# Expert stage: one buffer of transposed rows, three row and four result buffers, and the last scatters and late loads placed ahead of the branch of the full experts

## The chip, the cores and the metric

One core of one Trainium2 chip runs one program. The metric is the device time of one execution in microseconds (us); the time before is the median of 3 runs. PE is TensorE (PEld its weight loads), DVE VectorE, ACT ScalarE, POOL GpSimd, SP the engine that issues most DMAs; PEq, SPq and so on are the engines' sequencers, which run branches, semaphore instructions and DMA issues. L1322 is line 1322 of the kernel before.

## The reference

The reference is one inference step of a decoder with two layers on 576 tokens (512 of a prompt, 8 sequences of 8 samples), 1024 wide. Each layer normalizes and projects its input, runs three groups of recurrent heads (GLA, retention, Mamba-2), projects back with a residual and a norm, and then runs a mixture of experts: a token takes the best of 4 groups and the top 2 of the 4 experts in it. What the change touches is this last part, cut to its core:

```python
def hier_moe(h, l, p):
    ...
    top_v, top_i = lax.top_k(e_in, MOE_TOPK)
    ...
    hid = silu(einsum('nd,edf->nef', t, moe_w1[l])) * einsum('nd,edf->nef', t, moe_w3[l])
    y = einsum('nef,efd->nd', hid * combine[..., None], moe_w2[l])
...
x = layer_norm(ALPHA * x + g2 * hier_moe(h, l, p), ln2_g[l], ln2_b[l])
```

The kernel computes only the chosen experts of each token: 1152 rows (576 tokens times 2 choices) over 16 experts.

## The kernel before, in words

For each layer the kernel ranks the experts by how many rows they have and works through 16 **blocks**, one for each expert, from `experts` (L1819 on). A block b does, in this order: `gather` (L1322, POOL, an indirect DMA that brings its rows from hbuf to a row buffer X); `turn` (L1334 or, for the blocks in LIGHT, L1417: PE transposes the rows, and ACT and DVE copy them from PSUM into the transposed rows, as a high part xh, L1340, and a low part xl, L1341; light blocks have one plain copy xf, L1418); `up` twice (L1353, L1425); `hid` (L1363, L1434, a transpose of the hidden values); `down` (L1373, L1442), whose results ACT (L1375, L1443) and DVE (L1377) scale into a result buffer ys; and `scatter` (L1384, POOL, an indirect DMA from ys to the rows of ybuf in HBM). The weights of an expert are three pieces of 1 MB that SP loads (L1286) into slots that go round by threes; for the blocks that aren't light ACT and DVE split the pieces of `up` into high and low parts (whi, L328; wlo, L329).

An expert with more rows than the block takes needs more work: a second part (`b2`, or `bx` for a light block) and a third (`b3`). They stand in branches on values that the ranking left in registers (L1985, L1996, L2006, L2010 and, for the third, L1907) and run or not by the data. In the loop over b (L1964 on) the step of block b holds `up` of block b, the branch with the parts of blocks b-1, b and b+1, `turn` of block b+1, the gather of block b+2, `down` and `scatter` of block b-1, and `hid` of block b. The framework derives the waits from what each instruction reads and writes and orders the instructions of each engine itself, near this order; `issue_after` holds an instruction behind another, `declare_no_dep` takes a wait away.

The buffers of the kernel before: the row buffers of the main blocks are two, X0 and X1, by b % 2, and those of the extra parts two more; the transposed rows xs and xf are two each, by b % 2; the result buffers yss are two, main blocks by b % 2, a second part the other one. The last two blocks, 14 and 15, write their results over X0 and X1 instead and keep them: `kept`.

The scatter of a block that isn't light is made by one of two POOL instructions behind a branch on POOL (L1935): all rows, or only 64 where that will do (SSPLIT, HALF). For blocks 14 and 15 those are 88 and 82 rows, as ROWS says.

After the loop there is one more branch, L2061, for experts with still more rows (`nx > 0`, up to 4 full blocks). In this profile it isn't taken in either layer. Then comes `combine`: for each of five tiles of 128 tokens (tile 4 has 64) `pre` (L2106) adds, with PE, the two rows that the experts left for each token, read back from ybuf by `take` (L1894, two DMAs for each tile, SP); then DVE and ACT do residual and norm (L2118 to L2126). The tiles 0 and 1 are EARLY: they are read from ybuf before the last two scatters, and what blocks 14 and 15 add for them comes through PE, from `kept` and a mask `hot` (loaded from the constants at L1861, finished by DVE at L1870), in place of ybuf. For that ybuf's rows of these two tiles are zeroed at the start of each layer (L577, from bz). The other three tiles, 4, 2 and 3, are the late loads, 2.5 MB in six DMAs, behind the branch L2061; and as the body of this branch may change ybuf, it has loads of the EARLY tiles of its own. PE's first `pre` so reads a tile that is written ahead of the branch and also in its body.

The order in which the branch and the late loads stand:

```python
            with tc.If(nx > 0), ExitStack() as sI:
                ...
                for t in EARLY:
                    take(t)
            if ahead:
                ahead.split()
            for t in CORDER:
                if t not in EARLY:
                    take(t)
```

Of the kernel before, what the change touches and what calls it, by code (L numbers as in the profile page):

```python
# [9 lines left out]
F32 = mybir.dt.float32  # L10
# [10 lines left out]
D = 1024  # L21
# [20 lines left out]
GSPLIT, SSPLIT = (9,), (0, 1, 2, 3, 4, 5, 6, 7, 8, 9, 10, 11, 12, 13, 14, 15)  # L42
# [118 lines left out]
def _body(nc, tc, a, ctx, dbg):  # L161
# [404 lines left out]
    def conv(l, S, hT, sp_):  # L566
# [7 lines left out]
        for t in EARLY:  # L574
            for k in range(2):
                o = PL * k + 128 * t
                sp.dma_start(ybuf[o:o + 128], bz.rearrange("p g t -> p (g t)")[:, 0:D])  # L577
# [1241 lines left out]
    def experts(last, finish, l, x, R, tabs, slots, rqk, rv, ahead):  # L1819
# [8 lines left out]
        with ExitStack() as sE:  # L1828
            third_ = mkpool(sE, "w3rd", side="right")
            ep = mkpool(sE, "ep", side="right")  # L1830
            Xs.append(ep.tile([128, D], F32, name="X3"))
            for X in Xs[:3]:
                pool.memset(X, 0.0)
            xs = [[ep.tile([128, KD, 128], F32R, name=f"x{c}{i}") for c in "hl"] for i in range(2)]
            xf = [ep.tile([128, KD, 128], F32, name=f"xf{i}") for i in range(2)]
            hids = [ep.tile([128, 2, 128], F32, name=f"hid{i}") for i in range(4)]
            sl2 = rv.rearrange("p t d -> p (t d)")[:, D:D + 256], lp.tile([128, 2, 128], F32, name="slp2", tag="gtanh", bufs=2)
            yss = [ep.tile([128, D], F32, name=f"ys{i}") for i in range(2)]
# [6 lines left out]
            def aside(b):  # L1845
                if 2 <= b < 2 + NT:
# [3 lines left out]
                    with tc.issue_after(bl[max(k for k in range(b + 2) if k not in GSPLIT)].got.ins):  # L1850
# [28 lines left out]
            def light(b, X, pl, part, y):  # L1879
                return Light(b, tabs, scat, X, xf[b % 2], hids[b % 2 if part == 0 else 2], y, sl if part == 0 else sl2, pl, part)  # L1880
            bl = [light(b, Xs[b % 2], psp, 0, yss[b % 2]) if b in LIGHT else
                  Block(b, tabs, scat, Xs[b % 2], xs[b % 2], hids[b % 2], (yss if b < NE - 2 else Xs)[b % 2], sl, psp, ROWS[b]) for b in range(NE)]

            kept = Xs[:2]
# [4 lines left out]
            def take(t):  # L1889

                n = tp_(t)
                if t not in ys:
                    ys[t] = wraw.tile([128, 2048], F32, name="wraw", tag="raw").rearrange("p (k n) -> p k n", k=2)
                loads[t] = [sp.dma_start(ys[t][:n, k], ybuf[PL * k + 128 * t:PL * k + 128 * t + n]) for k in range(2)]  # L1894


            bx = {b: light(b, Xs[2 + b % 2], psx, 1, yss[1 - b % 2]) for b in LIGHT}
            b2 = {b: Block(NE + b, tabs, scat, Xs[2 + b % 2], (xf if b in LIGHT else xs)[b % 2], hids[2], yss[1 - b % 2], sl2, psx, plain=b in LIGHT) for b in SECOND}
            b3 = {b: Block(2 * NE + b, tabs, scat, Xs[2 + (b + (b in SOON)) % 2], (xf if b in LIGHT else xs)[b % 2], hids[3], yss[b % 2 if b not in LIGHT else 1 - b % 2],
                           sl2, psx, plain=b in LIGHT) for b in THIRD}  # L1900
# [51 lines left out]
            steps = finish(Xs[3])  # L1952
# [3 lines left out]
            pool.memset(Xs[3], 0.0)  # L1956
# [7 lines left out]
            for b in range(NE + 1):  # L1964
# [12 lines left out]
                if b + 2 in GSPLIT:  # L1977
# [383 lines left out]
```

## Time and profile before

| | |
|---|---|
| time, median of 3 runs | 1463.41 us (1459.72 to 1465.74) |
| the profiled execution's own time | 1461.71 us |
| its span, first to last instruction | 1459.9 us |
| mean granted TensorE clock | 0.919 |
| DVE busy | 831.6 us (57%) |
| ACT busy | 488.2 us (33%) |
| POOL busy | 422.8 us (29%) |
| DMA | 267.40 MB, mean 183 GB/s |

The profile is of one execution, and its times count from the start of the span. A timeline row gives the start, the duration, the engine and line, the operation with what it writes and reads, how many instructions in a row it stands for, and in brackets how long the engine had been idle before it and what ended that. The expert stage of layer 0 lies at about 480 to 685 us, that of layer 1 at about 1160 to 1405 us; behind each follows its combine, and behind the second the end.

### The profile page before, as it was taken

The page shows a single profiled execution, that of the slowest core. Times are in us where ns is not written, and L with a number is a line of the kernel's source. Part 1 is how long each engine was busy: PE and PEld are TensorE (multiplying, and loading weights), DVE is VectorE, ACT ScalarE, POOL GpSimd, SP SyncE. Part 2 cuts the span into 40 slices and gives each one's busy share as a digit, 9 for nine tenths or more (in the row PEclk, how much of TensorE's full clock was granted, in tenths as well). Part 3 has the DMA queues.
Part 4 walks back from the last instruction along what each step waited for, and adds up shares of the span by engine and source line. Part 5 has one row for each costly group of instructions (what it writes and reads, how often), then busy time and mean ns, then how long its engine had stood idle before and what let it go on. Part 6 is the DMA issues. An engine that isn't in the chain of part 4 may idle for free. (4 is left out here: it accounts for less than half of the span.)

```text
span 1459.9 us, 22701 instructions
## 1 busy us (share of the span) xinstructions
PE 1240.8 (85%) x8166; PEld 935.4 (64%) x8166; DVE 831.6 (57%) x1905; ACT 488.2 (33%) x902; POOL 422.8 (29%) x354
## 2 busy tenths in 40 slices
PE   4999999998985798898879998889997577977983
PEld 0998677775774455575579896777576353545741
DVE  0576457446989442356858546536789733123647
ACT  0552133321343233353454233323134222223512
POOL 0014112215234543211432322233314354321105
PEclk7999999999987799999989998999998599998997
DMA  9545665865262747995525310018454363674742
GB/s 312 172 145 173 215 228 202 299 207 161 68 196 87 267 178 263 376 362 173 191 68 174 90 58 34 30 45 285 157 182 144 130 254 140 243 288 195 291 160 85
DMA packets 94704, 267.40 MB, mean 183 GB/s; under 512 B 24952, under 2 KB 53530, under 8 KB 75609
## 3 DMA queue, kind: packets, MB, share of 16 engines
q1 hardware_dynamic: 84600, 246.59, 47.9%
q0 software_dynamic: 9952, 18.86, 3.7%
q8 instruction: 86, 1.41, 0.4%
q14 instruction: 66, 0.53, 0.1%
HBM read 238.42 MB, written 38.90 MB: 190 GB/s over the span
## 5 line engine op out<-in xcount | busy, mean ns | idle before, releaser
L402 PE MATMUL ps<-whi,hT 128*128 128x256 f32 (+1 forms) x640 | 188.9, 295 | 7.8 <-ACT hT L493 7.0
L403 PE MATMUL ps<-wlo,hT 128*128 128x256 f32 (+1 forms) x640 | 183.8, 287 | 1.2 <-DVE wlo L329 1.2
L404 PE MATMUL ps<-whi,hT 128*128 128x256 f32 (+1 forms) x640 | 183.5, 287 | 0.2
L402 PEld LDWEIGHTS ps<-whi,hT 128*128 128x128 f32 (+1 forms) x640 | 116.7, 182 | 21.7 <-issue 10.8
L403 PEld LDWEIGHTS ps<-wlo,hT 128*128 128x128 f32 (+1 forms) x640 | 116.8, 182 | 3.8 <-issue 2.1
L404 PEld LDWEIGHTS ps<-whi,hT 128*128 128x128 f32 (+1 forms) x640 | 116.5, 182 | 1.8 <-DVE hT L494 0.9
L392 PE MATMUL ps<-hT,whi 128*128 128x288 f32 x512 | 89.4, 297 | 0.0
L329 DVE TENSOR_TENSOR wlo<-wraw,whi 128x2048 fp32r<-128x2048 f32 x30 | 68.6, 2287 | 33.3 <-ACT whi L328 33.1
L329 DVE TENSOR_TENSOR wlo<-w3rd,whi 128x2048 fp32r<-128x2048 f32 x22 | 66.1, 3036 | 25.1 <-ACT whi L328 25.1
L1353 PE MATMUL ps<-whi,xh 128*128 128x256 f32 x384 | 60.1, 300 | 21.8 <-ACT whi L328 6.7
L392 PEld LDWEIGHTS ps<-hT,whi 128*128 128x128 f32 x512 | 75.1, 188 | 0.4 <-ACT zdt L531 0.4
L265 PE MATMUL ada<-wada,scond 128*32 128x512 f32 x384 | 56.9, 665 | 19.3 <-DMA wada<-w_ada 19.3
L1562 PE MATMUL ps<-whi,mh 128*128 128x512 f32 (+1 forms) x160 | 69.8, 436 | 3.7 <-ACT mh L1548 3.7
L1322 POOL DMA_INDIRECT qk<-hbuf,srci x32 | 33.4, 1042 | 129.1 <-PE ps L1417 47.3
L1564 PE MATMUL ps<-whi,ml 128*128 128x512 f32 (+1 forms) x160 | 67.4, 425 | 2.9 <-DVE ml L1549 2.9
L1353 PEld LDWEIGHTS ps<-whi,xh 128*128 128x128 f32 x384 | 52.1, 202 | 26.7 <-DVE xl L1341 8.4
L1563 PE MATMUL ps<-wlo,mh 128*128 128x512 f32 (+1 forms) x160 | 68.9, 431 | 0.0
L1384 POOL DMA_INDIRECT ybuf<-ys,srci x20 | 21.0, 1051 | 163.9 <-DVE ys L1377 48.1
L328 ACT ACTIVATE whi<-wraw 128x2048 fp32r<-128x2048 f32 x30 | 57.3, 1911 | 16.8 <-PE ps L392 8.3
L842 POOL TENSOR_TENSOR qh<-qx,ex 128x256 f32<-128x256 f32 x32 | 31.3, 1008 | 99.9 <-issue 82.6
L1373 PE MATMUL ps<-w3rd,hid 128*128 128x512 f32 x128 | 59.8, 610 | 0.3
L1353 PE MATMUL ps<-wlo,xh 128*128 128x256 f32 x384 | 55.5, 289 | 2.2 <-DVE wlo L329 1.9
(551 smaller groups left out, 2891.6 us busy)
## 6 DMA issues: line engine op xcount, KB each, us to landing
wada<-w_ada SPq DMA_DIRECT2D x48, 1024.0 KB
wraw<-moe_w SPq DMA_DIRECT2D x36, 1024.0 KB
slots<-moe_w SPq DMA_DIRECT2D x30, 1024.0 KB
w3rd<-moe_w SPq DMA_DIRECT2D x30, 1024.0 KB
wraw<-w_in SPq DMA_DIRECT2D x22, 1024.0 KB
wraw<-w_out SPq DMA_DIRECT2D x8, 1024.0 KB
ybuf<-bz SPq DMA_DIRECT2D x8, 512.0 KB
hbuf<-g SPq DMA_DIRECT2D x8, 512.0 KB
```

The lines of the kernel that those rows point to most:

```text
L265: pe.matmul(acc[32 * q:32 * q + 32, :], sc_[:, k, :], w[:, o:o + 512], start=(k == 0), stop=(k == KD - 1))
L328: split.hi = act.activation(hi[:, :n], raw[:, :n], AF.Copy)
L329: dve.tensor_tensor(lo[:, :n], raw[:, :n], hi[:, :n].bitcast(F32), op=ALU.subtract)
L392: pe.matmul(p[:mw, :], lhs[:, k, m0:m0 + mw], rhs[:, k, 288 * h:288 * (h + 1)], start=(k == 0 and lhs is vh and rhs is hT[0]), stop=(k == ...
L402: pe.matmul(p[:n], hT[0][:, k, xs], vh[:, k, :], start=(k == 0), stop=False)
L403: pe.matmul(p[:n], hT[0][:, k, xs], vl[:, k, :], start=False, stop=False)
L404: pe.matmul(p[:n], hT[1][:, k, xs], vh[:, k, :], start=False, stop=(k == KD - 1))
L1353: pe.matmul(p, x[:, k], v[:, k], start=(x is self.xh and v is vh and k == 0), stop=(x is self.xl and k == KD - 1))
L1373: pe.matmul(p, self.hT[:, f], v[:, f, c], start=(f == 0), stop=(f == 1))
L1562: pe.matmul(p[:n], mh[:, k, :n], vh, start=(k == 0), stop=False)
L1563: pe.matmul(p[:n], mh[:, k, :n], vl, start=False, stop=False)
L1564: o = pe.matmul(p[:n], ml[:, k, :n], vh, start=False, stop=(k == 3))
```

## The change

The change does six things. (1) The transposed rows xs and xf have one buffer each for all parts. (2) The main blocks have three row buffers by b % 3 (the third in rv, where `hot` lies too) and the gathers are issued one block earlier; the extra parts have two (Xx). (3) Four result buffers: main blocks by b % 3, second parts the fourth, third parts (b + 2) % 3. (4) The scatters of blocks 14 and 15 leave the POOL branch and always take all their rows. (5) The late loads stand ahead of the branch L2061, which is issued behind the last scatter, and its body loads all five tiles again in place of two. (6) For that, layer 0 zeroes all five tiles of ybuf; layer 1 zeroes the EARLY ones, as before.

```diff
@@ -39,7 +39,7 @@
 ROWS = [min(128, 2 * T // max(r - 1, 1)) for r in RANK]
 
 HALF = [64 if r > 80 else r for r in ROWS]
-GSPLIT, SSPLIT = (9,), (0, 1, 2, 3, 4, 5, 6, 7, 8, 9, 10, 11, 12, 13, 14, 15)
+GSPLIT, SSPLIT = (9,), tuple(range(NE - 2))
 SECOND = [b for b in range(NE) if RANK[b] < 2 + 2 * T // 129]
 SOON = (2,)
 THIRD = [b for b in range(NE) if RANK[b] < 2 + 2 * T // 257]
@@ -571,10 +571,10 @@
         bz = sp_.tile([128, 2, T], F32, name="bz")
         pool.memset(bz, 0.0)
 
-        for t in EARLY:
+        for t in (ORDER, EARLY)[l]:
             for k in range(2):
                 o = PL * k + 128 * t
-                sp.dma_start(ybuf[o:o + 128], bz.rearrange("p g t -> p (g t)")[:, 0:D])
+                sp.dma_start(ybuf[o:o + tp_(t)], bz[:tp_(t)].rearrange("p g t -> p (g t)")[:, 0:D])
         cw = cp_.tile([128, 6, 5], F32, name="cw")
         sp.dma_start(cw, a["conv_w"][l])
         dve.tensor_scalar(cw, cw, 0.5, None, op0=ALU.mult)
@@ -1828,14 +1828,16 @@
         with ExitStack() as sE:
             third_ = mkpool(sE, "w3rd", side="right")
             ep = mkpool(sE, "ep", side="right")
-            Xs.append(ep.tile([128, D], F32, name="X3"))
-            for X in Xs[:3]:
+
+            Xm, Xx = Xs, [ep.tile([128, D], F32, name=f"X{i}") for i in range(2)]
+            for X in (*Xm, Xx[1]):
                 pool.memset(X, 0.0)
-            xs = [[ep.tile([128, KD, 128], F32R, name=f"x{c}{i}") for c in "hl"] for i in range(2)]
-            xf = [ep.tile([128, KD, 128], F32, name=f"xf{i}") for i in range(2)]
+
+            xs = [ep.tile([128, KD, 128], F32R, name=f"x{c}") for c in "hl"]
+            xf = ep.tile([128, KD, 128], F32, name="xf")
             hids = [ep.tile([128, 2, 128], F32, name=f"hid{i}") for i in range(4)]
             sl2 = rv.rearrange("p t d -> p (t d)")[:, D:D + 256], lp.tile([128, 2, 128], F32, name="slp2", tag="gtanh", bufs=2)
-            yss = [ep.tile([128, D], F32, name=f"ys{i}") for i in range(2)]
+            yss = [ep.tile([128, D], F32, name=f"ys{i}") for i in range(4)]
             w3rd = third_.tile([128, 3 * 2048], F32, name="w3rd")
             w3rd = [w3rd[:, 2048 * i:2048 * (i + 1)] for i in range(3)]
 
@@ -1847,7 +1849,7 @@
                     n, xt = tp_(b - 2), x[:tp_(b - 2), b - 2]
                     st = R["stat"][:n, b - 2]
                     act.activation(xt, xt, AF.Identity, scale=st[:, 1:2], bias=st[:, 2:3])
-                    with tc.issue_after(bl[max(k for k in range(b + 2) if k not in GSPLIT)].got.ins):
+                    with tc.issue_after(bl[max(k for k in range(min(b + 3, NE)) if k not in GSPLIT)].got.ins):
                         pool.tensor_tensor(xt, xt, ln1[:n, 0], op=ALU.mult)
                         pool.tensor_tensor(xt, xt, ln1[:n, 1], op=ALU.add)
                 if b == NE - 2 and ahead:
@@ -1877,11 +1879,11 @@
                         ahead.AB = feat_ab(l + 1, lp)
 
             def light(b, X, pl, part, y):
-                return Light(b, tabs, scat, X, xf[b % 2], hids[b % 2 if part == 0 else 2], y, sl if part == 0 else sl2, pl, part)
-            bl = [light(b, Xs[b % 2], psp, 0, yss[b % 2]) if b in LIGHT else
-                  Block(b, tabs, scat, Xs[b % 2], xs[b % 2], hids[b % 2], (yss if b < NE - 2 else Xs)[b % 2], sl, psp, ROWS[b]) for b in range(NE)]
-
-            kept = Xs[:2]
+                return Light(b, tabs, scat, X, xf, hids[b % 2 if part == 0 else 2], y, sl if part == 0 else sl2, pl, part)
+
+            kept = [Xm[(NE - 1) % 3 + 1], Xm[(NE - 1) % 3]]
+            bl = [light(b, Xm[b % 3], psp, 0, yss[b % 3]) if b in LIGHT else
+                  Block(b, tabs, scat, Xm[b % 3], xs, hids[b % 2], yss[b % 3] if b < NE - 2 else kept[b - NE + 2], sl, psp, ROWS[b]) for b in range(NE)]
             hot = rv.rearrange("p t d -> p (t d)")
             loads = {}
             ys = {t: slots[i].rearrange("p (k n) -> p k n", k=2) for i, t in enumerate(CORDER[2:])}
@@ -1894,10 +1896,10 @@
                 loads[t] = [sp.dma_start(ys[t][:n, k], ybuf[PL * k + 128 * t:PL * k + 128 * t + n]) for k in range(2)]
 
 
-            bx = {b: light(b, Xs[2 + b % 2], psx, 1, yss[1 - b % 2]) for b in LIGHT}
-            b2 = {b: Block(NE + b, tabs, scat, Xs[2 + b % 2], (xf if b in LIGHT else xs)[b % 2], hids[2], yss[1 - b % 2], sl2, psx, plain=b in LIGHT) for b in SECOND}
-            b3 = {b: Block(2 * NE + b, tabs, scat, Xs[2 + (b + (b in SOON)) % 2], (xf if b in LIGHT else xs)[b % 2], hids[3], yss[b % 2 if b not in LIGHT else 1 - b % 2],
-                           sl2, psx, plain=b in LIGHT) for b in THIRD}
+            bx = {b: light(b, Xx[b % 2], psx, 1, yss[3]) for b in LIGHT}
+            b2 = {b: Block(NE + b, tabs, scat, Xx[b % 2], xf if b in LIGHT else xs, hids[2], yss[3], sl2, psx, plain=b in LIGHT) for b in SECOND}
+            b3 = {b: Block(2 * NE + b, tabs, scat, Xx[(b + (b in SOON)) % 2], xf if b in LIGHT else xs, hids[3], yss[(b + 2) % 3], sl2, psx, plain=b in LIGHT)
+                  for b in THIRD}
 
             def two(b):
                 return tc.If((beyond & (1 << b)) > 0)
@@ -1949,11 +1951,12 @@
                 q.hid()
                 q.down()
                 q.scatter()
-            steps = finish(Xs[3])
+            steps = finish(Xx[0])
             next(steps)
             bl[0].turn()
             next(steps)
-            pool.memset(Xs[3], 0.0)
+            bl[2].gather()
+            pool.memset(Xx[0], 0.0)
             with tc.issue_after(last[0].ins), tc.issue_after(last[1].ins):
                 bl[0].up()
             for i in range(2):
@@ -1974,8 +1977,8 @@
                     bl[b + 1].split(0)
                 if b < NE and b not in LIGHT:
                     bl[b].up(1)
-                if b + 2 in GSPLIT:
-                    parts(b + 2, bl[b + 2].gather, True)
+                if b + 3 in GSPLIT:
+                    parts(b + 3, bl[b + 3].gather, True)
 
                 at_hand = [e for e in (b - 1, b, b + 1) if e in SECOND and e not in LIGHT or e == b and b in LIGHT]
                 if b in SECOND and b not in LIGHT:
@@ -2031,8 +2034,8 @@
                         load(b + 3, i)
                 if b + 1 < NE:
                     bl[b + 1].turn()
-                    if b + 2 < NE and b + 2 not in GSPLIT:
-                        bl[b + 2].gather()
+                    if b + 3 < NE and b + 3 not in GSPLIT:
+                        bl[b + 3].gather()
                     if b + 1 not in LIGHT:
                         bl[b + 1].split(1)
                         if b + 4 < NE:
@@ -2044,7 +2047,7 @@
                         for t in EARLY:
                             take(t)
                     st = parts(b - 1, bl[b - 1].scatter, b - 1 in SSPLIT)[0]
-                    if b > NE - 2:
+                    if b >= NE - 1:
                         for t in EARLY:
                             for o in loads[t]:
                                 tc.declare_no_dep(st.ins, o.ins, reason="other rows")
@@ -2057,14 +2060,17 @@
                 aside(b)
 
 
+            for t in CORDER:
+                if t not in EARLY:
+                    take(t)
             wr = slots[1]
-            with tc.If(nx > 0), ExitStack() as sI:
+            with tc.issue_after(st.ins), tc.If(nx > 0), ExitStack() as sI:
                 for j in range(NX):
                     if j == 0:
                         left_over(R, wr, tabs)
                     else:
                         sI.enter_context(tc.If(nx > j))
-                    q = Block(3 * NE + j, tabs, scat, Xs[3], xf[j % 2], hids[j % 2], yss[j % 2], sl, psx, plain=True)
+                    q = Block(3 * NE + j, tabs, scat, Xx[0], xf, hids[j % 2], yss[j % 2], sl, psx, plain=True)
                     e = sp.value_load(tabs[2][0:1, j:j + 1], min_val=0, max_val=NE - 1)
                     q.w = [wr] * 3
                     q.gather()
@@ -2077,13 +2083,12 @@
                     q.down()
                     q.scatter()
                 sI.close()
-                for t in EARLY:
+                first = dict(loads)
+                for t in CORDER:
                     take(t)
+                loads.update(first)
             if ahead:
                 ahead.split()
-            for t in CORDER:
-                if t not in EARLY:
-                    take(t)
         return g2, ys, loads, kept
 
     def combine(x, tail, rv, sG, leads):
```

## Rows read from the trace of the kernel before

**Rows 1.** The page, part 1: busy time of each engine, share, instructions.
```profile
PE 1240.8 (85%) x8166; PEld 935.4 (64%) x8166; DVE 831.6 (57%) x1905; ACT 488.2 (33%) x902; POOL 422.8 (29%) x354
```

**Rows 2.** The chain that ended last: start, duration, what.
```profile
1408.87 15.43 PE ps L2106 x32
```

**Rows 3.** The list of waits, PE: us in total, times, longest.
```profile
PE ps L1353 <- ACT whi L328: 6.7, 2, 3.9
...
PE ps L1353 <- ACT xh L1340: 6.1, 2, 3.2
...
PE ps L1334 <- DMA v<-hbuf,srci: 4.0, 1, 4.0
```

**Rows 4.** Timeline of layer 1's expert loop, ACT and PE, 1241 to 1341 us.
```profile
1241.22 0.69 ACT L1375 ACTIVATE ys<-ps,wslot 128x512 f32<-128x512 f32 x1 [12.51 <-DMA ybuf<-ys,srci]
...
1241.96 3.68 PE L1442 MATMUL ps<-wraw,hid 128*64 128x512 f32 x8 [10.17 <-ACT ys L1375]
...
1245.97 2.07 PE L1353 MATMUL ps<-whi,xh 128*128 128x256 f32 x8
...
1288.74 1.19 PE L1353 MATMUL ps<-whi,xh 128*128 128x256 f32 x8
...
1340.76 1.94 PE L1442 MATMUL ps<-wraw,hid 128*64 128x512 f32 x8
```

**Rows 5.** Timeline of layer 1's hand-over: SP, DVE, POOL and PE, 1405 to 1425 us.
```profile
1405.03 4.53 SPq L318 DMA_DIRECT2D ln<-ln  x2
1415.87 3.20 SPq L1894 DMA_DIRECT2D slots<-ybuf  x6
...
1405.04 0.75 DVE L1377 TENSOR_SCALAR qk<-ps,wslot 128x512 f32<-128x512 f32 x1 [3.64 <-PE ps L1373]
...
1413.76 0.90 POOL L1384 DMA_INDIRECT ybuf<-qk,srcf  x1 [6.06 <-DMA ln<-ln]
...
1408.87 3.40 PE L2106 MATMUL ps<-wraw,cst 128*128 128x512 f32 x4 [3.87 <-SPq L2061]
...
1424.22 2.36 PE L2106 MATMUL ps<-slots,cst 64*64 64x512 f32 x5
```

**Rows 6.** Line L2061 on SP in layer 1: duration ns, first and last start.
```profile
L2061 SPq COMPARE_BRANCH  x1: 45/45/45, 1405.4 to 1405.4; - x1
...
L2061 SPq EVENT_SEMAPHORE  x6: 17/17/17, 1408.8 to 1409.1; - x6
```

**Rows 7.** Timeline of layer 0's hand-over: SP, DVE, POOL and PE, 675 to 697 us.
```profile
675.80 1.76 SPq L1894 DMA_DIRECT2D wraw<-ybuf  x4
...
693.44 3.19 SPq L1894 DMA_DIRECT2D slots<-ybuf  x6
...
683.26 0.75 DVE L1377 TENSOR_SCALAR qk<-ps,wslot 128x512 f32<-128x512 f32 x1 [2.86 <-PE ps L1373]
...
690.78 0.90 POOL L1384 DMA_INDIRECT ybuf<-qk,srcf  x1 [5.29 <-DVE x L2120]
...
685.32 1.96 PE L2106 MATMUL ps<-wraw,cst 128*128 128x512 f32 x4 [2.10 <-PEq L2061]
```

**Rows 8.** Line L2061 on SP in layer 0: all nine counters, then the first six.
```profile
L2061 SPq EVENT_SEMAPHORE  x9: 17/17/17, 680.7 to 684.7; - x9
...
L2061 SPq EVENT_SEMAPHORE  x6: 17/17/17, 680.7 to 681.1; - x6
```

**Rows 9.** Timeline of SP at layer 0's zeroing, 85 to 120 us.
```profile
88.88 3.16 SPq L577 DMA_DIRECT2D ybuf<-bz  x4
101.39 0.38 SPq L381 DMA_DIRECT2D wraw<-w_in  x1
```

**Rows 10.** Busy time by stretch: us, PE, PEld, DVE, ACT, POOL, PEclk, DMA share, GB/s.
```profile
95.00:100.00 5.00, 5.00 (x40) 5.00 (x39) 4.87 (x10) 3.31 (x7) 1.10 (x4) 1.00 0.03 10
```

**Rows 11.** Timeline of layer 0: the load of hot (SP), the transposes of block 14 (PE).
```profile
643.34 0.34 SPq L1861 DMA_DIRECT2D v<-consts  x1
...
664.66 1.03 PE L1334 MATMUL ps<-cst,qk 128*128 128x128 f32 x8
```

## The prediction, made before the changed kernel ran

> **What bounds the kernel now.** The page's engine shares come first: PE is busy for 1240.8 us, 85% of the span [rows 1], so time is won only where PE stands still, and lost where something new makes it stand. The chain of waits comes next. It ends on PE's 32 matmuls of the combine (L2106) and then on DVE [rows 2], so whatever delays the first of these matmuls delays the end one for one. The list of PE's waits [rows 3] and the timelines round them give the three places that the change touches: one stop inside the expert loop of layer 1 [rows 4], and the hand-over from the experts to the combine, in layer 1 [rows 5, 6] and in layer 0 [rows 7, 8].
>
> In rows 4 PE stands for 10.17 us ahead of block 3's down (L1442) "<-ACT ys L1375". ACT itself had sat idle for 12.51 us until a scatter of ys had landed. The reader should see that two result buffers, shared by main, second and third parts of the blocks, are what stops PE: ACT may not write block 2's result before the scatter that still reads its buffer is through.
>
> In rows 6 SP meets the branch L2061 at 1405.4. The branch isn't taken, but SP then raises the counters that the body would have raised, the last six only at 1408.8 to 1409.1: by then the ln load that SP had issued at 1405.03 [rows 5] was 3.8 us old, which I read as its landing. So at a branch not taken SP still waits for its own transfers in flight; and PE, whose first combine matmul reads a tile that the body could have written, starts at 1408.87 after 3.87 us "<-SPq L2061" [rows 5]. The late loads (slots<-ybuf, x6, from 1415.87) stand behind the branch and cost nothing: PE's matmuls on slots follow at 1424.22 with no idle time ahead of them. In layer 0 four early loads, issued from 675.80 [rows 7], hold the last of nine counters back to 684.7 [rows 8], 8.9 us after the first issue, while PE starts at 685.32, released by its own branch.
>
> The profiled execution took 1461.71 us, span 1459.9 and 1.8 round it; it lies 1.7 us below the median of 1463.41. I sum against the profiled one. A difference of 0.5%, 7.3 us, is about what a measurement of this kernel can tell from none.
>
> **The change, part by part.** *Four result buffers.* Main blocks 2 and 3 and the second and third parts of block 2 now have different buffers, so the 10.17 us go. So does the slow clock behind the stop: eight matmuls of L1442 take 3.68 us behind it and 1.94 elsewhere, the next eight of L1353 2.07 and 1.19 [rows 4]; 1.7 + 0.9 = 2.6. What is late next: block 4's down uses the third part's buffer, whose scatter has landed by 1241.22, when ACT goes on, and that is about when PE would get there. Gain 12.8, bounds 8 and 15.
>
> *Row buffers, gathers a block earlier.* PE hardly waits for rows: 4.0 us in one place, for an extra block's (v<-hbuf) [rows 3], and those keep two buffers. 0, bounds 0 and a gain of 4. One more memset on POOL and one gather ahead of the loop lie beside PE's work.
>
> *One buffer of transposed rows.* The copies of block b+1 may now be written only when the second part of block b is through with them, behind its branch. Today that holds only for blocks two apart; PE waits for xh in two places, 6.1 us in all, at most 3.2 [rows 3]. It now holds for four more pairs (blocks 10 to 14) in each layer: bounds 0 and 8 x 3.2 = 25.6. Most of these branches stand beside a down, whose matmuls cover the copies, so I take 1.
>
> *The zeros.* Layer 0 writes ten pieces in place of four, 2.5 MB more. Four take SP 3.16 us, ten 7.9, to 96.8; its next issue comes at 101.39 [rows 9], and from 95 to 100 the queues carry 10 GB/s while PE is busy for 5.00 of 5.00 us [rows 10]. 0, bounds 0 and 2 if that next load slips. Without this cover ten issues would cost 4.7 more.
>
> *The hot load.* v<-consts, now at 643.34, must follow the transposes of block 14 at 664.66 [rows 11], as it overlaps their rows. Nobody on PE reads it before the combine: 0, bound 3 if loads queue behind it on SP.
>
> *Scatters and late loads ahead of the branch.* The last two scatters lose their POOL branch, and the last needn't wait behind L2061. That moves the late loads early, but they were hidden. What counts is SP: it must issue six loads, which wait for the last scatter to land, before it comes to the branch, and then waits for what is in flight before it raises PE's counters. Layer 0: DVE finishes ys(15) at 683.26 + 0.75 = 684.0 [rows 7]; the scatter follows 0.8 later (an estimate; one issue takes POOL 0.90 [rows 7]), at 684.8. From last scatter to first late load it is 2.7 us in layer 0 (690.78 to 693.44) and 2.1 in layer 1 (1413.76 to 1415.87) [rows 5, 7]; I take 2.1, to 686.9. The six issues take 3.2, to 690.1: the lower end is PE released right then, 4.8 later than 685.32. The upper end scales the 8.9 us of 2.0 MB to 11.1 for 2.5 MB and takes the 2.7: 698.6, 13.3 later. I take 8.9 from first issue to PE's counter, as with the early loads, since PE needs tile 0's counters, and these are among many: 695.8, **+10.5**. Layer 1: 1405.04 + 0.75 + 0.8 + 2.1 = 1408.7 [rows 5]; PE at 1417.6 in place of 1408.87, **+8.7**, ends +3.0 and +11.5. The clock: the first four matmuls of L2106 take 1.96 us in layer 0 behind a stop of 2.1, and 3.40 in layer 1 behind 3.87 [rows 5, 7], and a stop of ten cost 2.6 [rows 4]; so +2.6 in layer 0, and +1.2 in layer 1, which has lost 1.4 already. Together +23.0, bounds 10 and 29. The combine that follows has no slack to give it back [rows 2].
>
> Sum: -12.8 + 1.0 + 23.0 = +11.2, and 1461.7 + 11.2 = **1472.9**, 9.5 over the median, 0.65%.
>
> **The rivals.** *B, the loads land side by side.* The single 0.5 MB load of ln was back 3.8 us after its issue [rows 5, 6]. If the sixth late load is so too, issued 2.8 after the first, PE is released 6.6 after it: at 693.5 and 1415.3, +8.2 and +6.4. With the clock's 3.8 that makes 18.4; 18.4 - 12.8 + 1.0 = +6.6 gives 1468.3: no change that can be told. Against it, the early loads' last counter came 7.1 us after their last issue had ended (675.80 + 1.76) [rows 7, 8]. The Trainium skill, "DMA: Bandwidth & Descriptors", section "Anatomy of one DMA — SWDGE (gpsimd) path", fits one transfer by about 2.0 us fixed plus its bytes over 436 GB/s. By that, an estimate, the sixth load (256 KB) is back 2.6 us after its issue, the two moves are +7.0 and +5.2, and the time 1465.9; the early loads of this trace took longer than the page's fit.
>
> *A, the join is cheap: the other side.* PE's counters are among the first that SP raises, as six of nine were up at 681.1 in layer 0 [rows 8], and the free buffers also take away the 4.0 us for v<-hbuf and the longest wait for whi, 3.9 [rows 3]. Then 4.8 + 3.0 + 3.8 - 12.8 - 7.9 = -9.1, 1452.6: faster. For it, the order of the counters in the new branch isn't known; against it, in layer 1 PE started with the last six [rows 5, 6]. It decides where PE's first combine matmul comes within a us of SP's branch.
>
> *C, one buffer of transposed rows stalls the loop.* Half of the 25.6: 12 more, 1484.9. For it, waits of up to 3.2 us exist today where two blocks share; against it, PE has a down to put in front.
>
> *D, the loop gains nothing,* the change not doing what it says: the third part's buffer is main block 4's, and the stop moves there. 1461.7 + 1.0 + 23.0 = 1485.7.
>
> **How the numbers follow.** Forecast 0.33, B 0.23, A 0.25, C 0.11, D 0.08. A lies below the lower line (1456.1), B between the lines, the forecast, C and D above the upper one (1470.7): faster 0.25, same 0.23, slower 0.52. The range 1450 to 1487 takes in the centres of A, C and D; the forecast's own is 1462 to 1482, its tails' bounds used by half or more.
>
> **What the changed profile would show.** Right: no wait of ten us "<-ACT ys L1375" in layer 1's loop; the last scatter right behind ys(15), the late loads ahead of SP's COMPARE_BRANCH at L2061, and PE's first L2106 matmul waiting for some 10 us "<-SPq L2061" in both layers, its first four matmuls nearer to 3.40 us than to 1.96. Wrong: if L2106 starts within two us of where it does now, counted from ys(15); if SP raises the counters while its loads are in flight; or if blocks 10 to 14 show new waits "<-ACT xh L1340".

## The result and the profile after

The changed kernel takes 1482.45 us (1477.99 to 1485.97, 4 runs) against 1461.57 (1458.26 to 1465.74, 4 runs) for the kernel before, beside which it ran: ratio 1.014, 95% interval 1.01 to 1.018, so 20.9 us slower. The forecast was slower, 1472.9 in a range of 1450 to 1487. The profiled execution took 1485.97 us, 24.3 more than the one profiled before; the comparisons of stretches below are between these two.

The list of waits of the changed kernel, PE (us in total, times, longest), shows where the time is. L2067 is the branch that was L2061, L2111 the combine that was L2106, L1896 the loads that were L1894.

```profile
PE ps L2111 <- SPq L2067: 34.9, 2, 18.1
...
PE ps L1353 <- ACT xh L1340: 12.8, 4, 3.3
...
PE ps L1353 <- DVE xl L1341: 6.5, 12, 1.0
...
PE ps L1334 <- issue: 3.7, 1, 3.7
```

The first line is new in size: PE waits 34.9 us for SP's branch, 18.1 us in one of the two layers. In [rows 3, 5, 7] there were 3.9 us on this line, and 2.1 for PE's own branch. The 10.2 us of L1442 "<-ACT ys L1375" are gone from the list. The waits for xh have doubled, as [rows 3] made one expect of a single buffer, but the 6.7 us for whi of [rows 3] are gone, so these two lines cancel. It is the same place, block 11, in the kernel before and then in the changed one, layers 0 and 1 (the starts of the two kernels differ by what comes ahead):

```profile
622.90 2.60 PE L1353 MATMUL ps<-whi,xh 128*128 128x256 f32 x10 [2.80 <-ACT whi L328]
1346.98 2.60 PE L1353 MATMUL ps<-whi,xh 128*128 128x256 f32 x10 [3.91 <-ACT whi L328]
```

```profile
627.61 2.08 PE L1353 MATMUL ps<-whi,xh 128*128 128x256 f32 x8 [3.28 <-ACT xh L1340]
1356.31 1.22 PE L1353 MATMUL ps<-whi,xh 128*128 128x256 f32 x8 [3.29 <-ACT xh L1340]
```

The hand-over of layer 0 in the changed kernel's timeline, engine by engine, and under it the instructions of the branch on SP. This answers to [rows 7, 8].

```profile
692.62 3.18 SPq L1896 DMA_DIRECT2D slots<-ybuf  x6
695.89 0.56 SPq L433 DMA_DIRECT2D wraw<-w_in  x1
696.50 3.01 SPq L434 DMA_DIRECT2D wraw<-w_in  x1
...
688.04 1.42 POOL L1384 DMA_INDIRECT ybuf<-qk,srcf  x1 [1.22 <-DVEq L2067]
...
686.38 0.75 DVE L1377 TENSOR_SCALAR qk<-ps,wslot 128x512 f32<-128x512 f32 x1 [2.80 <-PE ps L1373]
...
704.46 3.75 PE L2111 MATMUL ps<-wraw,cst 128*128 128x512 f32 x4 [18.12 <-SPq L2067]
...
720.85 3.64 PE L2111 MATMUL ps<-slots,cst 64*64 64x512 f32 x8
```

```profile
L2067 SPq EVENT_SEMAPHORE  x9: 17/17/17, 700.0 to 704.4; - x9
...
L2067 SPq COMPARE_BRANCH  x1: 45/45/45, 699.6 to 699.6; - x1
```

Read it from DVE down: the last result is ready at 686.38 + 0.75, its scatter starts 0.9 us later, the late loads 4.6 us after that, SP comes to its branch at 699.6, and its last counter goes up at 704.4, 11.8 us after the first late load was issued. The core's DMA traffic falls to 0 GB/s at 703.6, 0.8 us ahead of this last counter. PE starts 0.1 us after the counter, and its first four matmuls take 3.75 us, where they took 1.96 [rows 7]: the granted clock of this stretch is 0.50, the lower of the two levels (1.2 GHz), and was 1.00 (2.4 GHz) before. Ahead of it PE had stood for 18.12 us, and for 2.10 before.

Layer 1, the same two views ([rows 5, 6]):

```profile
1422.35 3.55 SPq L1896 DMA_DIRECT2D slots<-ybuf  x6
...
1417.54 1.41 POOL L1384 DMA_INDIRECT ybuf<-qk,srcf  x1 [3.45 <-issue]
...
1415.88 0.75 DVE L1377 TENSOR_SCALAR qk<-ps,wslot 128x512 f32<-128x512 f32 x1 [3.64 <-PE ps L1373]
...
1432.62 3.75 PE L2111 MATMUL ps<-wraw,cst 128*128 128x512 f32 x4 [16.78 <-SPq L2067]
...
1448.45 1.93 PE L2111 MATMUL ps<-slots,cst 64*64 64x512 f32 x4
```

```profile
L2067 SPq EVENT_SEMAPHORE  x9: 17/17/17, 1426.4 to 1432.6; - x9
...
L2067 SPq COMPARE_BRANCH  x1: 45/45/45, 1426.0 to 1426.0; - x1
```

It is 4.8 us from scatter to load and 10.25 us from the first load to the last counter; the traffic ends at 1431.9, 0.7 us ahead of that counter. With these starts the span can be cut into stretches that can be compared; the first transposes of each layer's block 0, where the expert loop starts, are these, of the kernel before and of the changed one:

```profile
479.00 1.11 PE L1417 MATMUL ps<-cst,qk 64*128 64x64 f32 x8 [2.60 <-DMA qk<-hbuf,srci]
1156.65 1.12 PE L1417 MATMUL ps<-cst,qk 64*128 64x64 f32 x8 [1.02 <-DMA qk<-hbuf,srci]
```

```profile
483.14 1.11 PE L1417 MATMUL ps<-cst,qk 64*128 64x64 f32 x8 [2.71 <-DMA qk<-hbuf,srci]
...
1174.34 1.11 PE L1417 MATMUL ps<-cst,qk 64*128 64x64 f32 x8 [1.12 <-DMA qk<-hbuf,srci]
```

| stretch, us | before | after | difference |
|---|---|---|---|
| start to block 0, layer 0 | 479.0 | 483.1 | +4.1 |
| expert loop, layer 0, to the last DVE result | 204.3 | 203.2 | -1.0 |
| last result to first combine matmul, layer 0 | 2.1 | 18.1 | +16.0 |
| first combine matmul to first one on slots | 13.9 | 16.4 | +2.5 |
| on to block 0, layer 1 | 457.4 | 453.5 | -3.9 |
| expert loop, layer 1 | 248.4 | 241.5 | -6.9 |
| last result to first combine matmul, layer 1 | 3.8 | 16.7 | +12.9 |
| first combine matmul to first one on slots | 15.4 | 15.8 | +0.5 |
| to the end | 35.7 | 35.8 | +0.1 |

Differences are taken before rounding. The two hand-overs cost 31.9 us with the slow clock in them, the two loops bring 7.9. The first and the fifth row can't be told from chance: over the profiles of all kernels of this study block 0 of layer 0 starts between 479 and 486 us, whatever is in them, and the fifth row swings by as much.

### The profile page after: what moved, and what is told of

The parts are those of the page before. It is cut to its first block, busy times and chain, and to the rows that moved or that the text cites. A ratio compares the mean times of both kernels' runs of the same rounds, so it can differ in the third digit from the quotient of the medians.

```text
span 1484.2 us, 22671 instructions
## 1 busy us (share of the span) xinstructions
PE 1253.4 (84%) x8166; PEld 945.5 (64%) x8166; DVE 826.4 (56%) x1905; ACT 487.7 (33%) x902; POOL 430.1 (29%) x356
## 5 line engine op out<-in xcount | busy, mean ns | idle before, releaser
L329 DVE TENSOR_TENSOR wlo<-wraw,whi 128x2048 fp32r<-128x2048 f32 x30 | 68.6, 2287 | 33.0 <-ACT whi L328 32.8
L1353 PE MATMUL ps<-whi,xh 128*128 128x256 f32 x384 | 60.5, 302 | 22.0 <-ACT xh L1340 12.8
L328 ACT ACTIVATE whi<-wraw 128x2048 fp32r<-128x2048 f32 x30 | 57.3, 1910 | 18.1 <-PE ps L392 8.3
L392 PE MATMUL ps<-hT,wlo 128*128 128x288 f32 x256 | 55.0, 296 | 0.0
```

The lines of the kernel that those rows point to most:

```text
L328: split.hi = act.activation(hi[:, :n], raw[:, :n], AF.Copy)
L329: dve.tensor_tensor(lo[:, :n], raw[:, :n], hi[:, :n].bitcast(F32), op=ALU.subtract)
L392: pe.matmul(p[:mw, :], lhs[:, k, m0:m0 + mw], rhs[:, k, 288 * h:288 * (h + 1)], start=(k == 0 and lhs is vh and rhs is hT[0]), stop=(k == ...
L1353: pe.matmul(p, x[:, k], v[:, k], start=(x is self.xh and v is vh and k == 0), stop=(x is self.xl and k == KD - 1))
```

## Experiments

**The late loads put back, and put ahead alone.** The first kernel undoes one part of the change, the second does this part alone on the kernel before.

```
late_back, against the changed kernel:
-            for t in CORDER: if t not in EARLY: take(t)        (ahead of the branch)
-            with tc.issue_after(st.ins), tc.If(nx > 0), ...
+            with tc.If(nx > 0), ...
-                for t in CORDER: take(t)                       (in the body)
+                for t in EARLY: take(t)
+            for t in CORDER: if t not in EARLY: take(t)        (behind the branch)
-        for t in (ORDER, EARLY)[l]:                            (the zeros)
+        for t in EARLY:

late_ahead, against the kernel before: the same lines the other way round,
and SSPLIT = tuple(range(NE - 2))
```

> Late loads behind the branch again, with the branch's body loading the EARLY tiles alone and layer 0 zeroing these alone; the buffers, the earlier gathers and the undivided last scatters stay. Theory W (the whole loss is PE's wait for SP's counters at the branch not taken): PE's two waits on SP's branch fall from 18.1 and 16.8 us to under 5 us each, the loop keeps its gain of about 8 us, and the time is 1453 to 1456 us. Rival U (the undivided scatters and the single buffer of transposed rows cost as much as they bring): 1460 to 1470 us.

> The kernel before with the late loads ahead of the branch alone (the zeros, the two undivided scatters and the ten loads in the body, which it needs, included); buffers and gathers as before. Theory W: PE waits 16 to 19 us on SP's branch in both layers and the time is 1486 to 1492 us, above the changed kernel, as the loop's gain is missing; the 10.2 us stop in layer 1's loop is there. Rival U: the tails cost only about half of it without the new buffers, 1470 to 1476 us.

With the loads back, 1457.08 us against 1465.74 for the kernel before: ratio 0.9938 (0.9915 to 0.9961), faster. With the loads ahead alone, 1498.49: 1.0226 (1.0204 to 1.0248), or 32.8 us slower. The waits are as theory W had them in both; the times lie above its ranges, by 1.1 and 6.5 us, which were set when the kernel before had measured 1461.6 (here it is 1465.7). The 32.8 us agree with the 31.9 of the two hand-overs in the table. The list of waits of late_ahead, PE, has the long wait and still the stop of the loop:

```profile
PE ps L2108 <- SPq L2064: 35.9, 2, 18.0
...
PE ps L1442 <- ACT ys L1375: 9.6, 1, 9.6
```

In late_back PE waits 1.9 us in layer 0 between its last matmul and the combine, and the stretches to the first combine matmul are 1.9 and 1.5 us. The two loops gain 2.3 and 7.0 us in its profile.

**The zeros alone**, on the kernel before (for t in (ORDER, EARLY)[l] at L574 and tp_(t) rows in each transfer).

> The kernel before with layer 0 zeroing all five tiles, ten transfers in place of four. Theory W with the prediction's cover: within 2 us of the kernel before (1460 to 1464 us). Rival Z (the 4 us by which the changed kernel's profile is later at the first expert block, ahead of anything else that was changed, come from these transfers): 1465 to 1467 us.

1464.87 against 1465.74, ratio 0.9992 (0.9973 to 1.0012): no difference. In the one profile of it block 0 starts at 485.8, the latest of all, but after_win below has the same zeros and starts it the earliest, at 478.8. The 4.1 us ahead of block 0 are not the zeros'.

**What PE waits for: the body's writes, or the loads?** The changed kernel without the reloads in the body, then the changed kernel and the kernel before without the branch.

```
no_reload:       -                for t in CORDER: take(t)     (in the body, all ten loads)
after_nobranch:  -            with tc.issue_after(st.ins), tc.If(nx > 0), ... and its whole body
before_nobranch: -            with tc.If(nx > 0), ... and its whole body
```

> The changed kernel with the body of the branch leaving out its ten loads (a part of the computation that this data doesn't reach). Theory W: PE's first combine matmul no longer reads anything that the body writes, so it starts within 3 us of the last down in both layers while SP still stands at its branch: 1450 to 1457 us. Rival L (it is the late loads and the last scatter's landing that hold PE, whatever the branch raises): 1470 us or more.

> The changed kernel with the whole branch of the full experts left out (a part of the computation that this data doesn't reach), the late loads where the change put them. Theory W (the branch not taken, with the late loads in flight ahead of it, is the whole loss): PE starts the combine within 1 us of the last down in both layers, waits for late loads at most a few us later, and the time is 1448 to 1455 us. Rival L (the earlier late loads, the undivided scatters or the gathers cost something of their own): 1460 us or more.

> The kernel before with the same branch left out. Theory W: it loses its two stops of 2.1 and 3.9 us at the branch and the slow clock behind the second, 1.4, so it is 5 to 8 us faster than the kernel before. Rival: the late loads then come too late for PE, as the last scatter holds them, and the gain is under 3 us.

no_reload took 1478.42, ratio 1.0099 (1.0077 to 1.0121). Theory W's first half came true and its time didn't; the time is that of rival L. The combine's PE timeline of no_reload in layer 1:

```profile
1408.74 1.88 PE L2107 MATMUL ps<-wraw,cst 128*128 128x512 f32 x4
...
1419.13 1.93 PE L2107 MATMUL ps<-slots,cst 64*64 64x512 f32 x4
1430.08 2.04 PE L2107 MATMUL ps<-slots,cst 128*128 128x512 f32 x2 [9.03 <-SPq L2067]
```

The first matmul follows the last down with no gap, but a later one, on another tile of slots, waits 9.03 us for the same branch: the body still loads weights into slots[1]. In layer 0 it is 7.69 us in the same place. The wait had only moved to the next tile that the body writes, and PE came to it with some of the combine done. So the reader of a tile is held here if anything in the body writes the tile, a reload or another load.

Without the branch the question is settled. after_nobranch took 1446.0 against 1466.6, ratio 0.9866 (0.9837 to 0.9894); before_nobranch 1452.67, ratio 0.9907 (0.9876 to 0.9938). The hand-over of layer 0 in after_nobranch, SP and PE:

```profile
688.75 3.18 SPq L1896 DMA_DIRECT2D slots<-ybuf  x6
...
682.32 1.88 PE L2087 MATMUL ps<-wraw,cst 128*128 128x512 f32 x4
...
696.14 3.64 PE L2087 MATMUL ps<-slots,cst 64*64 64x512 f32 x8
```

The late loads, the undivided scatters and the early gathers are all in it, and PE neither stops nor slows down: the loads land while PE does its eight groups of matmuls on the early tiles. What is slow in the changed kernel is the branch not taken together with the loads ahead of it, about 40 us between these two kernels (1.014 against 0.9866), and theory W stands (the time lies 2 us below its range). The branch costs the kernel before something too. Its two profiles differ by 7.9 us of span (1459.9 and 1452.0), at the upper end of what was expected; the runs say 9 to 18, and what the rest is isn't known.

**Which term of the hand-over was too small.** The first kernel divides the last two scatters again, the second takes two small loads from between the late loads and the branch.

```
after_split, against the changed kernel:
-SSPLIT = tuple(range(NE - 2))
+SSPLIT = (0, 1, ... 14, 15)
-            with tc.issue_after(st.ins), tc.If(nx > 0), ...
+            with tc.issue_after(loads[CORDER[-1]][-1].ins), tc.If(nx > 0), ...

after_win, against the changed kernel (what the next layer's loads are issued behind):
-            yield t, mu, rstd, b, o, loads[CORDER[-1]][-1]
+            yield t, mu, rstd, b, o, firsts[0]                 (the combine's first matmul)
```

> The changed kernel with its last two scatters divided again on POOL (64 rows or all), the late loads still ahead of the branch. Theory P (two more microseconds of each hand-over than the prediction had are the undivided scatter, which lands in 4.6 to 4.8 us and not in 2.1 to 2.7): the late loads follow the last scatter after 2 to 3 us, PE's two waits on SP's branch are 16 and 15 us, and the time falls by 3 to 5 us. Rival: the landing stays at 4.6 us or the POOL branch costs as much; no difference.

> The changed kernel with the two narrow loads of the next layer's w_in no longer between the late loads and the branch on SP (they go out ahead of the late loads, while SP waits for the last scatter). Theory Q (in layer 0 SP came to the branch 3.7 us later because of them): the wait of layer 0 falls from 18.1 to 13 to 15 us, that of layer 1 stays at 16.8, and the time falls by 3 to 6 us. Rival: the landings of the late loads, not SP's arrival at the branch, set it: layer 0 stays within 1 us of 18.1.

after_split: 1477.46, 1.0112 (1.0068 to 1.0156); after_win: 1486.51, 1.0172 (1.0129 to 1.0214). Neither can be told from 1.014 by its time; the rows tell more. The last scatter and the first late load in after_split, layer 0, then layer 1:

```profile
688.56 3.18 SPq L1896 DMA_DIRECT2D slots<-ybuf  x6
...
685.60 0.91 POOL L1384 DMA_INDIRECT ybuf<-qk,srcf  x1 [1.06 <-DVEq L2069]
```

```profile
1407.03 0.81 SPq L318 DMA_DIRECT2D ln<-ln  x2
1413.50 3.19 SPq L1896 DMA_DIRECT2D slots<-ybuf  x6
...
1408.53 0.90 POOL L1384 DMA_INDIRECT ybuf<-qk,srcf  x1 [3.48 <-DVEq L2069]
```

Divided, the scatter of layer 0 needs 3.0 us to the load, not 4.6, and PE's wait there is 15.9 us; that part of theory P holds. Whether it is the number of rows or how the transfer is cut up isn't told apart: from the scatter to the load the profile counts 80 packets of the software queue with the divided scatter and 672 in the changed kernel, for the same 0.04 MB. In layer 1 it is 5.0 us although it is divided (PE's wait is 17.4 us, not 15), so there the size isn't the cause. Two ln loads of 0.5 MB each are issued 1.5 us ahead of this scatter; in the kernel before the scatter came late enough (1413.76 [rows 5]) to find them landed. That they hold it up is likely and was not tried by itself, but the other profiles agree. In layer 1 a divided last scatter needs 2.1 us in six kernels, where the second ln load was issued 4 us or more ahead of it (the kernel before, zeros_only, xs1, xs1_ys4, late_back_split, late_back_g2_split), and 4.3 us in before_nobranch, where it was 2.6 us or less. after_win, SP in layer 0 and its counters:

```profile
687.40 3.18 SPq L1896 DMA_DIRECT2D slots<-ybuf  x6
...
L2067 SPq EVENT_SEMAPHORE  x9: 17/17/17, 691.1 to 698.6; - x9
L2067 SPq COMPARE_BRANCH  x1: 45/45/45, 690.6 to 690.6; - x1
```

SP reaches the branch right behind the sixth load, and still the last counter goes up 11.2 us after the first. PE's wait is 17.5 us in place of 18.1. The traffic ends at 698.2, 0.4 us ahead of the last counter. Theory Q falls and the rival holds: the landing of the late loads sets the counter, and SP's arrival is hidden under it.

**The buffers.** One part, then two, on the kernel before:

```
xs1:      xs = [[x for "hl"]] * 2 and xf = [xf] * 2: one buffer each, used for both parities
xs1_ys4:  xs1, and
-            yss = [... for i in range(2)]
+            yss = [... for i in range(4)]     (main b % 3, second parts 3, third (b + 2) % 3)
```

> The kernel before with one buffer of transposed rows (xs and xf) in place of two, and nothing else. Theory N (the copies wait, but only where PE waited for split weights anyway): PE's wait for xh grows from 6.1 us to some 12 us, its wait for whi falls by as much, and the time is within 2 us of the kernel before. Rival C of the prediction: slower by 6 us or more.

> The kernel before with one buffer of transposed rows and four result buffers (two main row buffers, gathers, scatters, branch and late loads as before). Theory Y (the result buffers alone take away the 10.2 us stop and the slow clock behind it, and the gathers a block earlier gave back a part): 10 to 13 us faster than the kernel before, the stop at block 3's down gone and no 3.7 us stop at the second part of block 5. Rival: 5 to 8 us faster, as the changed kernel's loop, so that the rest lies in something else, such as the clock.

xs1 took 1472.0 against 1463.86: 1.0059 (1.0035 to 1.0083), slower by some 8 us. Theory N's waits came as expected and its time didn't: the time is rival C's, for this part by itself. xs1_ys4 took 1453.73: 0.9927 (0.9897 to 0.9957), 10 us faster, the 10.2 us stop gone and no stop of 3.7 us, as theory Y had it. Its profile doesn't show where all of this lies: it is of the slowest of seven executions (1461.48), and there the loops gain 0.0 and 5.1 us. Four result buffers can't be had without the single buffer (there is no room), so what they bring alone wasn't tried. The lists of waits, PE, of xs1 and then of xs1_ys4:

```profile
PE ps L1353 <- DVE xl L1341: 13.8, 12, 1.8
PE ps L1353 <- ACT xh L1340: 12.9, 4, 3.5
```

```profile
PE ps L1353 <- ACT xh L1340: 12.7, 4, 3.3
...
PE ps L1353 <- DVE xl L1341: 6.7, 12, 1.0
```

The waits for xh are the same in both, and balanced by those for whi that are gone. What only xs1 has are 7 us more for xl, 6.3 of them at blocks 13 and 14 of both layers (1.84 us each, where xs1_ys4 has 0.26). Just ahead of these, ACT's next whi waits for PE's counter at the loop's own branch, L1985, in xs1 for 4.16 us and in xs1_ys4 for 2.54:

```profile
646.72 1.91 ACT L328 ACTIVATE whi<-slots 128x2048 fp32r<-128x2048 f32 x1 [4.16 <-PEq L1985]
```

```profile
645.82 1.91 ACT L328 ACTIVATE whi<-slots 128x2048 fp32r<-128x2048 f32 x1 [2.54 <-PEq L1985]
```

The two kernels differ in the result buffers alone, so these shorten that wait; by what step isn't shown.

**Scatters and gathers**, with the late loads back: the scatters divided again; and besides, the gathers at b + 2 again, with three row buffers.

```
late_back_split, against late_back:     SSPLIT as in the kernel before
late_back_g2_split, besides:
-                    if b + 3 < NE and b + 3 not in GSPLIT:
-                        bl[b + 3].gather()
+                    if b + 2 < NE and b + 2 not in GSPLIT:
+                        bl[b + 2].gather()                     (and the other places alike)
```

> The changed kernel with the late loads behind the branch and the last two scatters divided again (64 rows or all). Theory S (an undivided scatter of 82 rows lands in 4.5 us, a divided one in 2.5, hidden behind PE's first combine matmuls once the loads are behind the branch): within 2 us of the same kernel with undivided scatters, 0.994 of the kernel before. Rival: 4 to 6 us faster than that one, 0.990, the combine of layer 0 being free of the gap of 5 us between its first and its ninth group of matmuls.

> As the kernel with late loads behind the branch and divided scatters, and with the gathers at their old place, a block later, in three row buffers. Theory G (the earlier main gather and the products behind it stand ahead of the extra parts' gathers on POOL, which made PE stop 3.7 us for the second part of block 5 in layer 1 and run slowly behind it): that stop is gone and the time is 4 to 7 us below the kernel with early gathers. Rival: no difference, the stop only moves.

1459.22, 0.9958 (0.9935 to 0.998), and 1457.06, 0.9952 (0.9928 to 0.9976), beside 0.9938 for late_back: none of the three can be told apart, so the 4 to 6 us of the rival to theory S are not there (its 2 us are finer than these intervals). Of theory G the stop is as expected, the time isn't. late_back_split has this line in PE's timeline of layer 1, and late_back_g2_split none of its kind:

```profile
1266.39 1.94 PE L1334 MATMUL ps<-cst,X 128*128 128x128 f32 x8 [3.46 <-issue]
```

and yet the loop of layer 1 takes 238.3 us with it and 237.5 without. The rival, that the stop only moves, fits: late_back_g2_split lost its time earlier. Near the start of the loop PE waits at a loop branch (L1999 in late_back_split, L1998 in late_back_g2_split), in late_back_split and then in late_back_g2_split:

```profile
1185.55 0.99 PE L1334 MATMUL ps<-cst,v 128*128 128x128 f32 x7 [3.56 <-PEq L1999]
```

```profile
1186.60 1.76 PE L1334 MATMUL ps<-cst,v 128*128 128x128 f32 x7 [4.93 <-PEq L1998]
```

The wait is 1.4 us longer and the matmuls behind it are slower. PE comes to the transposes right ahead of the place of the stop 98.7 us after the loop's start with the stop and 102.0 without, 3.3 us later. What makes that earlier wait longer is open.

## Why the prediction was right, and where its terms were off

The mechanism and the sign were right; the size was about half. Summed from the profiles it was to be +11.2 and was +24.3. That 1482.45 lies in the stated range is in part luck: it is above the forecast's own 1462 to 1482, and the range reaches further only for rivals C and D, whose mechanisms didn't make this time. Both large terms missed the same way: the hand-overs with the clock cost 31.9, not 23.0, and more than their bound of 29; the loops brought 7.9, not 11.8.

- **Four result buffers, -12.8.** The stop of [rows 4] and the slow matmuls behind it went: in the changed kernel block 3's down follows the transposes directly, 75.8 us after block 0's first transposes, where it was 85.3, so 9.5 us sooner. But the loop of layer 1 is only 6.9 us shorter. A stop of 3.7 us "<-issue" stands at a second part's transposes, followed by slow matmuls (granted clock 0.54 from 1279 to 1286). The bounds were 8 to 15; both loops together brought 7.9.

```profile
1249.13 1.09 PE L1334 MATMUL ps<-cst,v 128*128 128x128 f32 x8
1250.15 1.94 PE L1442 MATMUL ps<-wraw,hid 128*64 128x512 f32 x8
...
1279.05 1.53 PE L1334 MATMUL ps<-cst,X 128*128 128x128 f32 x8 [3.67 <-issue]
```

- **Row buffers and early gathers, 0.** The runs show no gain from them, and no loss that can be measured.
- **One buffer of transposed rows, 1.** Too little by itself: 8 us, which don't show once there are four result buffers. The step left out the loop's branch, where ACT waits for PE's counter (4.16 us in xs1). The prediction's own sign of being wrong, new waits "<-ACT xh L1340" in blocks 10 to 14, did come, 3.3 us at block 11 in each layer; they cost nothing because PE had waited there for whi before.
- **The zeros, 0; the hot load, 0.** That of the zeros is shown; for the load no kernel was run.
- **The hand-overs, +10.5 and +8.7,** were mis-sized: +16.0 and +12.9. Two terms make the difference. From the last scatter to the first late load I took 2.1 us, from divided scatters with little else under way; it is 4.6 and 4.8. From the first late load to the last counter I took the 8.9 us of four early loads; it is 11.8 and 10.25. The upper end of 11.1, scaled by the bytes, lies between the two, and the argument for the lower one (PE needs only a few of the counters) was the wrong step: PE started with the last of nine in both layers. 2.5 + 2.9 and 2.7 + 1.35, with the scatter's start 0.1 later, are the missing 5.5 and 4.2. Both hand-overs lie above their upper ends, +13.3 and +11.5, as these took 2.7 us for the scatter.
- **The clock, +3.8.** It is 3.0 by the stretches behind the first matmul (2.5 and 0.5).
- **The rivals.** B falls, as six loads of 2.5 MB don't land side by side: the last counter comes 8.0 us after the sixth issue has ended in after_win (687.40 + 3.18 to 698.6). The fit of the Trainium skill, "DMA: Bandwidth & Descriptors", section "Anatomy of one DMA — SWDGE (gpsimd) path", gave 2.6 us for a sixth load of 256 KB. But in the trace the first two loads have 256 KB and the sixth 512 KB: by the fit, an estimate, 3.2 us, and a time of 1467.1 in place of 1465.9. The page gives this fit for the queue of POOL, and these loads are SP's. Taken for all 2.5 MB as one transfer it is 2.0 + 6.0 = 8.0 us, an estimate, and the runs show 10.25 to 11.8 us. A falls: the counter that PE needed came last, not first. C is right for the single buffer alone, without the four result buffers. D falls: no stop of ten us is left in the loop.

## What to carry to other kernels

Before anything that loads is moved ahead of a conditional branch, ask what the path not taken must wait for: here the queue's engine raised the counters that the body would have raised only when its own loads in flight had landed, and the reader of a tile that the body writes waited with it. Whether the framework or the chip sets this wait the rows don't tell. In these kernels loads that nobody needed soon were better off behind the branch, and what they cost ahead of it was the landing of all their bytes, not of the tile that was needed. The buffers without the move, late_back (0.9938) or just xs1_ys4 (0.9927), are faster than both kernels.

## What the runs showed of the hardware that was not expected

In late_back PE stops for 2.20 us in the middle of a tile's matmuls behind the branch not taken in layer 0, for nothing that the profile shows, and runs slowly after it (four matmuls in 3.62 us, not 1.88; the granted clock is 0.50 from 689.1 to 694.5, and 1.00 ahead of the stop):

```profile
685.83 1.10 PE L2109 MATMUL ps<-wraw,cst 128*128 128x512 f32 x2 [1.93 <-PEq L2064]
689.12 2.04 PE L2109 MATMUL ps<-wraw,cst 128*128 128x512 f32 x2 [2.20 <-issue]
690.96 3.62 PE L2109 MATMUL ps<-qk,v 128*128 128x512 f32 x4
```

That makes the stretch to the first matmul on slots 19.2 us in place of 13.9 in the kernel before, 5.3 us more, so part of what the move back regains is lost again. Stops like it, of 1.2 to 2.3 us, appear in xs1, xs1_ys4, late_back_split and late_back_g2_split too, but not in the kernel before or zeros_only, and not in the two without the branch. The Trainium skill, "Runtime: NRT & Kernel Launch", section "Instruction fetch mechanics", says that a taken branch to a place outside what is prefetched makes the engine wait for a fetch. No run here shows that this is the cause: the profile counts the packets of two instruction queues, and in late_back one lies at 686.2 to 686.6, right ahead of the stop, and none in it; but the kernel before, which doesn't stop, has one in the same place, at 686.0 to 686.4. The five kernels with such a stop have one more of these packets 1 to 2 us after its end, the kernel before and zeros_only have none there; whether that is a cause or a consequence isn't shown, and the cause stays open.
